# Encoder trunk on one core: moving weights of the 512-column products stored with even columns first and read as two streams

## The chip, the cores and the metric

The kernel runs on one core of a Trainium2 chip. The metric is the device time of that core in microseconds (us), from its first to its last instruction, with what little lies around them. TensorE multiplies; ScalarE (ACT in the rows), VectorE (DVE), GpSimd (POOL) and the DMA queues feed it and take its sums away.

## The reference

A trunk of two layers over 256 tokens of width 2048 with 256 memory tokens. Each layer has a token mixer with 12 heads and a cross-attention with 4 heads, one output projection, and an MLP of width 8192 with a squared ReLU. Cut to what matters here:

```python
for i in range(DEPTH):                                   # DEPTH = 2
    n = rms_norm(h, attn_norm[i])
    z = n @ a_w_in[j]     # layer 0; layer 1: n @ b_w_in[j]
    ...
    km, vm = jnp.split(m @ w_mem_kv[i], 2, axis=-1)
    ...
    h = h + jnp.concatenate([mix, cross], axis=-1) @ w_o[i]
    n = rms_norm(h, mlp_norm[i])
    h = h + jnp.square(jax.nn.relu(n @ w_up[i])) @ w_down[i]
return rms_norm(h, final_norm)
```

All of it is float32. Every dense product `n @ w` is what the change can touch; the attention itself is small beside them.

## The kernel before

Each float32 operand of a product is held as a pair, hi and lo: hi is the number rounded to float32r (a 4-byte format that TensorE multiplies in one go), lo the rest. A product is three matmuls: hi by hi, hi by lo, lo by hi. `split` (line 454; its instructions carry lines 456 and 457) makes a pair with one ACT copy and one DVE subtraction.

A matmul holds a stationary operand of 128x128 in the array and streams a moving operand through it, one column after another; each column of the moving operand gives one column of the sum in PSUM. There are two kinds of product:

- **S products** (`products`, line 350, matmul on line 362): the weights are stationary, the activations move, 256 columns (the tokens) at a time. Q and K of layer 0, the memory keys and the whole of the up projection (`up_grains`) are made so.
- **M products** (`m_products`, line 330, matmuls on lines 339, 342 and 343): 128 tokens of the activations are stationary, the weights move, 512 columns at a time. V of layer 0, the memory values, all of layer 1's input projection, the output projection and the last part of the down projection (`plain_grains`) are made so. The rest of the down projection (`down_grains`, its `run`, lines 1149, 1151 and 1152) has the same shape: it multiplies blocks by Strassen's seven products p1 to p7, with `th`/`tl` (four blocks that are sums of weights) and `bh`/`bl` (three blocks of the weights) as moving operands.

One chunk of weights is 128 partitions by 2048 columns (1 MB, `CH`), that is four blocks of 512. It is laid out on the host by `m_chunks`, `pair_chunks` and `plain_chunks`, so that a block of 512 columns lies in order in 2048 bytes of each partition. A chunk is loaded by SP's queue, split by ACT and DVE (in halves of two blocks, or four blocks `th`/`tl` and three blocks `bh`/`bl`), and read block by block by TensorE.

The constants `MOVING_AT`, `STILL_AT`, `U_AT`, `ENTRY_AT`, `LAST_AT` and so on shift single tiles by 32 to 384 bytes in the partition. The sequence of the work is set by `run_all`: a list of grains, each with a load, a preparation and a run, and with the number of grains by which load and preparation go ahead of the run. In the MLP one step is: three Strassen products with `bh`/`bl` (9 matmuls of 512 columns), an up chunk (48 matmuls of 256 columns), four Strassen products with `th`/`tl` (12 matmuls of 512). There are 58 such steps in each layer.

Two places read a moving operand that isn't one run: in layer 1's attention the keys (`Far.part`, line 132, read by lines 512 to 514) come as 8 runs of 32 columns, 512 bytes apart from start to start; and on lines 653 to 655 four runs of 64.

## Time and profile before

| | |
|---|---|
| time, median of 3 runs | 1989.95 us (1989.51 to 1990.23) |
| profiled execution, span from first to last instruction | 1988.4 us |
| TensorE busy | 1980.1 us, 100% of the span, 12838 matmuls |
| TensorE weight loads | 1799.3 us, 90% (beside the matmuls) |
| VectorE busy | 1717.0 us, 86% |
| ScalarE busy | 1339.5 us, 67% |
| GpSimd busy | 140.6 us, 7% |
| DMA engines | mean 226 GB/s |

Busy shares overlap. A matmul's record reaches from its start to the modelled end of its pipeline, so two records in a row lie over each other: the mean of 390 ns for a matmul of 512 columns isn't what it costs. What it costs is the distance from its start to the start of the next one, which the timeline view shows.

### The profile page before, as it was taken

What the parts mean: (1) busy time and instruction counts of PE and PEld (TensorE: products, weight loads), DVE (VectorE), ACT (ScalarE), POOL (GpSimd) and SP (SyncE); (2) the same over time, 40 slices, a digit from 0 to 9 for tenths busy, and PEclk for the clock granted to TensorE, in tenths of its full rate; (3) what the DMA queues carried; (4) which work ended last, traced back from release to release, by engine and by line L of the source; (5) the groups of instructions that cost most, each with busy time, mean ns of one, the idle gap of its engine ahead of it and who ended that gap; (6) DMA issues with size and microseconds to landing.
All of it is one profiled execution on the core that took longest, in us unless ns stands there. A gap on an engine that the chain in (4) does not pass through costs nothing.

```text
span 1988.4 us, 32806 instructions
## 1 busy us (share of the span) xinstructions
PE 1980.1 (100%) x12838; PEld 1799.3 (90%) x12838; DVE 1717.0 (86%) x2131; ACT 1339.5 (67%) x1892; POOL 140.6 (7%) x179
## 2 busy tenths in 40 slices
PE   9999999999999999999999999999999999999998
PEld 8999999899999999999998888889999999999997
DVE  7777777589898999999999778788998999999998
ACT  6655555477777777777766658677776777777674
POOL 0000000000000000000000001000000000000000
PEclk9999999999999999999999999999999999999999
DMA  7856655767777777777766765667777777777772
GB/s 291 320 192 207 200 192 185 270 194 241 234 234 227 230 233 238 234 227 234 216 228 204 255 226 177 207 218 250 237 223 237 226 228 236 234 238 228 225 232 111
DMA packets 117339, 448.52 MB, mean 226 GB/s; under 512 B 24640, under 2 KB 49984, under 8 KB 69824
## 3 DMA queue, kind: packets, MB, share of 16 engines
q1 hardware_dynamic: 99168, 415.12, 59.5%
q0 software_dynamic: 17728, 30.78, 9.7%
q8 instruction: 101, 1.65, 0.3%
q10 hardware_dynamic: 288, 0.52, 0.1%
q14 instruction: 54, 0.44, 0.1%
HBM read 397.78 MB, written 4.19 MB: 202 GB/s over the span
## 4 chain that ended last, share of the span: by engine, by line
PE 99%; issue 0%; DVE 0%; POOL 0%; DVEq 0%; ACT 0%; POOLq 0%; ACTq 0%
PE ps_u L362 35%; PE ps_s L362 10%; PE p L1149 9%; PE p L1152 9%; PE p L1151 9%; PE ps_m L343 8%; PE ps_m L339 8%; PE ps_m L342 8%; PE av L653 0%; PE sc_ps L513 0%; PE av L654 0%; PE sc_ps L514 0%; PE sc_ps L512 0%; PE av L655 0%; PE idle L236 0%
## 5 line engine op out<-in xcount | busy, mean ns | idle before, releaser
L362 PE MATMUL ps_u<-hT,uh 128*128 128x256 f32 x3812 | 662.9, 276 | 0.0
L362 PEld LDWEIGHTS ps_u<-hT,uh 128*128 128x128 f32 x3812 | 578.7, 188 | 5.5
L362 PE MATMUL ps_u<-hT,ul 128*128 128x256 f32 x1960 | 541.5, 276 | 0.0
L456 ACT ACTIVATE uh<-raw_U 128x1024 fp32r<-128x1024 f32 x262 | 276.8, 1058 | 208.0 <-PE ps_u L362 193.1
L362 PEld LDWEIGHTS ps_u<-hT,ul 128*128 128x128 f32 x1960 | 368.0, 188 | 0.0
L457 DVE TENSOR_TENSOR lo<-raw,hi 128x1024 fp32r<-128x1024 f32 (+1 forms) x215 | 254.3, 1189 | 92.2 <-ACT hi L456 91.1
L457 DVE TENSOR_TENSOR ul<-raw_U,uh 128x1024 fp32r<-128x1024 f32 x262 | 318.9, 1221 | 16.2 <-ACT uh L456 16.2
L457 DVE TENSOR_TENSOR tl<-t,th 128x2048 fp32r<-128x2048 f32 x116 | 265.7, 2290 | 70.4 <-ACT th L456 70.0
L456 ACT ACTIVATE hi<-raw 128x1024 fp32r<-128x1024 f32 (+1 forms) x215 | 222.0, 1038 | 143.0 <-PE ps_m L343 73.9
L456 ACT ACTIVATE th<-t 128x2048 fp32r<-128x2048 f32 x116 | 222.8, 1920 | 117.4 <-PE p L1152 112.5
L457 DVE TENSOR_TENSOR bl<-b,bh 128x1536 fp32r<-128x1536 f32 x116 | 203.3, 1753 | 0.0
L1149 PE MATMUL p<-th,a_s 128*128 128x512 f32 x464 | 181.3, 391 | 0.0
L1118 POOL DMA_DIRECT2D t<-b x116 | 100.6, 868 | 1139.4 <-ACT t L1117 1057.7
L1151 PE MATMUL p<-tl,a_s 128*128 128x512 f32 x464 | 181.0, 390 | 0.0
L1152 PE MATMUL p<-th,a_s 128*128 128x512 f32 x464 | 180.6, 389 | 0.0
L456 ACT ACTIVATE bh<-b 128x1536 fp32r<-128x1536 f32 x116 | 172.3, 1485 | 7.8
L362 PE MATMUL ps_s<-nT,hi 128*128 128x256 f32 x896 | 154.7, 277 | 0.0
L1152 PE MATMUL p<-bh,a_s 128*128 128x512 f32 x348 | 136.2, 391 | 0.0
L362 PEld LDWEIGHTS ps_s<-nT,hi 128*128 128x128 f32 x896 | 135.5, 188 | 0.1
L1149 PE MATMUL p<-bh,a_s 128*128 128x512 f32 x348 | 135.4, 389 | 0.0
L1151 PE MATMUL p<-bl,a_s 128*128 128x512 f32 x348 | 135.4, 389 | 0.0
L362 PE MATMUL ps_s<-nT,lo 128*128 128x256 f32 x448 | 124.2, 277 | 0.0
(303 smaller groups left out, 3591.0 us busy)
## 6 DMA issues: line engine op xcount, KB each, us to landing
raw_U<-in_w_up SPq DMA_DIRECT2D x128, 1024.0 KB, 5.8
b<-in_w_pair SPq DMA_DIRECT2D x116, 1024.0 KB, 5.8
raw<-in_w_o SPq DMA_DIRECT2D x32, 1024.0 KB, 5.0
t<-b POOLq DMA_DIRECT2D x116, 256.0 KB, 5.1
raw<-in_w_b SPq DMA_DIRECT2D x21, 1024.0 KB, 5.9
raw<-in_w_av SPq DMA_DIRECT2D x12, 1024.0 KB, 5.0
raw<-in_w_aq SPq DMA_DIRECT2D x12, 1024.0 KB, 4.9
raw<-in_w_ak SPq DMA_DIRECT2D x12, 1024.0 KB, 4.9
```

The costliest lines, as they stand in the source:

```text
L339: first = nc.tensor.matmul(ps, ah, hi[:, s], start=st, stop=False)
L342: nc.tensor.matmul(ps, ah, lo[:, s], start=False, stop=False)
L343: final = nc.tensor.matmul(ps, al, hi[:, s], start=False, stop=sp)
L362: ins = nc.tensor.matmul(ps, x, acts[:, k, part], start=k == n == 0, stop=k == KT - 1 and n == 2)
L456: first = nc.scalar.activation(dst_hi, src, AF.Copy)
L457: return first, nc.vector.tensor_tensor(dst_lo, src, dst_hi.bitcast(F32), op=ALU.subtract)
L1118: nc.gpsimd.dma_start(s[:, 3, :], b[:, 1, :], accum_op=ALU.add)
L1149: ins = nc.tensor.matmul(ps, a[:, 0, ai, :], hi[:, s], start=begins, stop=False)
L1151: nc.tensor.matmul(ps, a[:, 0, ai, :], lo[:, s], start=False, stop=False)
L1152: nc.tensor.matmul(ps, a[:, 1, ai, :], hi[:, s], start=False, stop=ends)
```

## The change

The three host functions that lay out moving weights store each block of 512 columns with its even columns first: place i of the block holds column 2i, place 256 + i holds column 2i + 1 (`evens_first`). The matmuls read the block by `in_turn`: place 0, place 256, place 1, place 257, and so on, so that the columns come to the array in their old order, 0, 1, 2, 3, and the sums in PSUM lie where they lay. The access pattern of the moving operand was one run of 512 elements of 4 bytes; it is now 256 times two elements, 1024 bytes apart, 4 bytes further each time. `pairs` gives PSUM's side the same shape; in the program that is built it is still one run of 512.

All 4524 matmuls of 512 columns are changed, and the 48 of 256 columns with which the last block of the kernel is made in two parts (`part`). S products, splits, loads, tile places and sizes are as before, and every engine has the same instructions in the same order with the same names.

```diff
+    def pairs(x):
+        return x.rearrange("p (i b) -> p i b", b=2)
+
+    def in_turn(x, begin=0, end=512):
+
+        return x.rearrange("p (b i) -> p i b", b=2)[:, begin // 2 : end // 2, :]
+
...
-        ps = w.ps[i if bank is None else bank][:, part[0] : part[1]]
+        ps = pairs(w.ps[i if bank is None else bank][:, part[0] : part[1]])
         for j in range(nk):
-            s = slice(j * 512 + part[0], j * 512 + part[1])
+            mh, ml = (in_turn(x[:, j * 512 : (j + 1) * 512], *part) for x in (hi, lo))
             ah, al = acts(k0 + j, i)
             st, sp = begins and j == 0, ends and j == nk - 1
-            first = nc.tensor.matmul(ps, ah, hi[:, s], start=st, stop=False)
+            first = nc.tensor.matmul(ps, ah, mh, start=st, stop=False)
             if keep_order:
                 pin(first)
-            nc.tensor.matmul(ps, ah, lo[:, s], start=False, stop=False)
-            final = nc.tensor.matmul(ps, al, hi[:, s], start=False, stop=sp)
+            nc.tensor.matmul(ps, ah, ml, start=False, stop=False)
+            final = nc.tensor.matmul(ps, al, mh, start=False, stop=sp)
...
-                ps, s = box["ps"][name], slice(bi * 512, (bi + 1) * 512)
-                ins = nc.tensor.matmul(ps, a[:, 0, ai, :], hi[:, s], start=begins, stop=False)
+                ps = pairs(box["ps"][name])
+                mh, ml = (in_turn(x[:, bi * 512 : (bi + 1) * 512]) for x in (hi, lo))
+                ins = nc.tensor.matmul(ps, a[:, 0, ai, :], mh, start=begins, stop=False)
                 pin(ins)
-                nc.tensor.matmul(ps, a[:, 0, ai, :], lo[:, s], start=False, stop=False)
-                nc.tensor.matmul(ps, a[:, 1, ai, :], hi[:, s], start=False, stop=ends)
+                nc.tensor.matmul(ps, a[:, 0, ai, :], ml, start=False, stop=False)
+                nc.tensor.matmul(ps, a[:, 1, ai, :], mh, start=False, stop=ends)
...
+def evens_first(x):
+
+
+    return x.reshape(*x.shape[:-1], 256, 2).swapaxes(-1, -2).reshape(x.shape)
...
-    return np.ascontiguousarray(x).reshape(-1, P, CH)
+    return np.ascontiguousarray(evens_first(x)).reshape(-1, P, CH)
```

The last pair of lines is from `m_chunks`; `pair_chunks` and `plain_chunks` are changed in the same way.

## Rows read from the trace of the kernel before

**Rows 1.** The page's head: span, busy times, the chain that ended last.

```profile
span 1988.4 us, 32806 instructions
PE 1980.1 (100%) x12838; PEld 1799.3 (90%) x12838; DVE 1717.0 (86%) x2131; ACT 1339.5 (67%) x1892; POOL 140.6 (7%) x179
PE 99%; issue 0%; DVE 0%; POOL 0%; DVEq 0%; ACT 0%; POOLq 0%; ACTq 0%
```

**Rows 2.** Whom TensorE waited for: line waiting, releaser, total us, times, longest.

```profile
PE idle L236 <- POOL mhalf L231: 1.0, 1, 1.0
```

**Rows 3.** Whole span, matmuls of line 1149, then of line 339 (window, its length, busy (count)).

```profile
0.00:1988.40 1988.40, 316.69 (x812) 152.58 (x812) 1.00 0.70 226
...
0.00:1988.40 1988.40, 269.53 (x712) 133.68 (x712) 1.00 0.70 226
```

**Rows 4.** Groups of TensorE, forms of line 339 with 256 columns (count, busy, mean).

```profile
L339 PE MATMUL ps_m<-uh,a_s 128*128 128x256 f32 x8 | 2.2, 280 | 0.0
L339 PE MATMUL ps_m<-h_p,a_p 128*128 128x256 f32 x8 | 2.2, 279 | 0.0
```

**Rows 5.** Timeline of TensorE, an MLP step's 21 Strassen matmuls (start us, length, line).

```profile
950.72 0.40 PE L1149 MATMUL p<-th,a_s 128*128 128x512 f32 x1
950.95 0.39 PE L1151 MATMUL p<-tl,a_s 128*128 128x512 f32 x1
951.18 0.39 PE L1152 MATMUL p<-th,a_s 128*128 128x512 f32 x1
...
955.26 0.40 PE L1152 MATMUL p<-bh,a_s 128*128 128x512 f32 x1
955.50 0.28 PE L362 MATMUL ps_u<-hT,u 128*128 128x256 f32 x1
```

**Rows 6.** Timeline of TensorE, 24 matmuls of an up chunk, first and next after.

```profile
444.17 0.39 PE L362 MATMUL ps_u<-hT,uh 128*128 128x256 f32 x2
...
446.89 0.39 PE L362 MATMUL ps_u<-hT,uh 128*128 128x256 f32 x2
```

**Rows 7.** Timeline of TensorE, layer 1: 24 matmuls with `Far` keys, moving in 8 runs.

```profile
1194.04 0.28 PE L512 MATMUL sc_ps<-kT,qT 128*128 128x256 f32 x1
...
1196.91 0.40 PE L343 MATMUL ps_m<-hi,nT 128*128 128x512 f32 x1
```

**Rows 8.** Timeline of TensorE, layer 0: 4 matmuls with memory keys in one run.

```profile
111.46 0.28 PE L514 MATMUL sc_ps<-km,qmT 128*128 128x256 f32 x1
...
111.93 0.28 PE L362 MATMUL ps_s<-nT,hi 128*128 128x256 f32 x1
```

**Rows 9.** Timeline of TensorE, start: 20 plain float32 matmuls of 128 columns.

```profile
0.98 4.63 PE L236 MATMUL idle<-ones 128*128 128x128 f32 x20 [0.98 <-POOL mhalf L231]
5.27 0.70 PE L362 MATMUL ps_s<-memT,hi 128*128 128x256 f32 x2
```

**Rows 10.** Groups of VectorE: transposes by input pattern, and splits (count, busy, mean ns).

```profile
L492 DVE STREAM_TRANSPOSE rows<-mem_col 128x256 f32<-128x256 f32 x1 | 0.4, 447 | 0.0
L565 DVE STREAM_TRANSPOSE sc_t<-sc 128x256 f32<-128x256 f32 x40 | 23.2, 618 | 0.6 <-ACT sc L526 0.6
L547 DVE STREAM_TRANSPOSE h_t<-h_t 128x512 f32<-128x512 f32 x8 | 8.2, 1103 | 0.0
L457 DVE TENSOR_TENSOR ul<-raw_U,uh 128x1024 fp32r<-128x1024 f32 x262 | 318.9, 1221 | 16.2 <-ACT uh L456 16.2
L457 DVE TENSOR_TENSOR tl<-t,th 128x2048 fp32r<-128x2048 f32 x116 | 265.7, 2290 | 70.4 <-ACT th L456 70.0
```

**Rows 11.** Stretches of the MLPs: length, busy PE, PEld, DVE, ACT, POOL, clock, DMA.

```profile
500.00:960.00 460.00, 460.00 (x3105) 422.38 (x3105) 424.24 (x436) 329.44 (x386) 40.05 (x46) 1.00 0.74 232
970.00:1030.00 60.00, 60.00 (x404) 54.98 (x403) 59.51 (x67) 42.65 (x52) 4.35 (x5) 1.00 0.73 231
1400.00:1900.00 500.00, 500.00 (x3373) 459.04 (x3373) 462.57 (x478) 358.00 (x421) 42.24 (x49) 1.00 0.74 231
1900.00:1970.00 70.00, 70.00 (x426) 62.44 (x425) 68.70 (x78) 44.48 (x57) 2.58 (x3) 1.00 0.54 182
```

**Rows 12.** Timeline of VectorE in that step: the split of `th`.

```profile
955.60 2.29 DVE L457 TENSOR_TENSOR tl<-t,th 128x2048 fp32r<-128x2048 f32 x1 [1.18 <-ACT th L456]
```

More of the change, by code (lines that the diff above doesn't have):

```diff
@@ L1588, in pair_chunks @@
     x = x.reshape(-1, 2, P, 4, 512)[:, :, :, [3, 0, 2, 1]]
-    return np.ascontiguousarray(x).reshape(-1, P, CH)
+    return np.ascontiguousarray(evens_first(x)).reshape(-1, P, CH)
 def plain_chunks(w):
@@ L1595, in plain_chunks @@
     x = [x[nb, c] for nb in REST for c in chunks_left(nb)]
-    return np.ascontiguousarray(np.stack(x)).reshape(-1, P, CH)
+    return np.ascontiguousarray(evens_first(np.stack(x))).reshape(-1, P, CH)
 def by_feature(x):
```

## The prediction

> **What bounds the kernel now.** I read the head of the page first, then the list of TensorE's waits, then the timeline. TensorE is busy in the whole span, the chain that ended last is TensorE for 99% of it [rows 1], and the only wait listed for it is 1.0 us at the start [rows 2]. So no other engine sets the time; the sum of the distances between matmul starts does. The question is then what one matmul costs, and a mean duration doesn't tell it, since records overlap. The timeline does: in one MLP step 20 matmuls of 512 columns lie between the starts 950.72 and 955.26 [rows 5], which is 4.54 / 20 = 0.2270 us for each. An up chunk's 24 matmuls of 256 columns take 446.89 - 444.17 = 2.72 us [rows 6], 113.3 ns each.
>
> The granted clock in the stretches of the MLP is 1.00, which is the 2.4 GHz level [rows 11]. One column in each cycle would be 512 / 2.4 = 213.3 ns and 256 / 2.4 = 106.7 ns. Both shapes lose the same share: 227.0 / 213.3 = 1.064 and 113.3 / 106.7 = 1.062, or one cycle for every 16 columns (17/16 = 1.0625). The loss grows with the columns, so it isn't a price of starting a matmul nor of a weight load, of which there is one for either shape. It sits in the stream of columns. The 20 plain float32 matmuls at the start go from 0.98 to 5.27 [rows 9], 214.5 ns for 128 columns, which is 512 whole cycles of 2.4 GHz and 1.2 ns: four cycles for a column, and no seventeenth (that would be 226.7). There a column of 4 bytes is wanted only every fourth cycle; here every cycle. So I take the loss for one of reading the moving operand: the reader can't quite bring 4 bytes per partition in each cycle. That is an inference from two rates, not something a row says.
>
> **What the change does, part by part.** No instruction is added, removed or moved, and no DMA: the host stores the same bytes in another order. The splits of ACT and DVE read and write the same runs. What changes is how 4572 matmuls read: 3 x 812 in the Strassen part and 3 x 712 in the other M products [rows 3], of which 3 x 16 = 48 have 256 columns [rows 4]. That leaves 4524 with 512 columns, 4524 x 0.2270 = 1027 us, 52% of the span. A nanosecond more or less on each is 4.5 us, or 0.23%.
>
> No row of the trace shows a moving operand read from two places in turn, so its price has to be bounded from both sides. The lower end is one column per cycle, 213.3 ns: the stream can't be faster than the array takes it, which excludes more than a gain of 13.7 ns. The upper end is what VectorE pays when each element lies in another place: its transposes that read elements 16 bytes apart take 1103 ns for 512 and 618 for 256, so 1.89 ns for each [rows 10], where its split takes (2290 - 1221) / 1024 = 1.04 ns for an element in a run [rows 10]. At 1.89 ns a block of 512 takes 970 ns, 743 ns more than now. In between lies TensorE's own nearest row, the one on jumps: keys in 8 runs of 32 columns, 512 bytes apart, take 2.87 / 24 = 119.6 ns [rows 7], keys in one run (111.93 - 111.46) / 4 = 117.5 ns [rows 8]. Seven jumps cost 2.1 ns at most, 0.3 ns each, less than a cycle. The reader thus follows the pattern of the instruction and not the neighbourhood in memory, and a far line costs it about what the next line costs.
>
> I take a value near the lower end. If a far line is as good as the next one, what loses the seventeenth cycle is that the next piece of a single run isn't there in time: it is wanted 16 columns after the last. With two streams in turn each piece lasts twice as long, and the piece that follows it has twice the time to come. For this the reader has to keep one piece of each stream at hand while it takes from the other. That is the weak point of the forecast; nothing above shows that it can.
>
> The sum: 4524 x (227.0 - 213.3) = 62 us at most. From it come off: (a) a fixed price of a start, now hidden in the lost cycles perhaps, 1.2 ns by the plain matmuls [rows 9], 4524 x 1.2 = 5 us. (b) VectorE as the next bound. In the steady part of the MLP it is busy 424.24 of 460 us and 462.57 of 500 [rows 11], 92%. A step of 48 x 113.3 + 21 x 227.0 = 10.2 us gets 21 x 12.5 = 0.26 us shorter, 2.6%, and VectorE's share goes to 95%: it still fits. The tightest link, `tl`, ends at 955.60 + 2.29 = 957.89 [rows 12], and its product starts 48 x 113.3 ns after 955.50 [rows 5], at 960.94: 3 us of cover, of which the change takes a tenth or so. But at the end of each layer VectorE is full: 59.51 of 60 us and 68.70 of 70 [rows 11]. There TensorE can't go faster than VectorE, so the gain of those 130 us is lost at worst, 2.6% to 5.5% of it (the higher in the part with M products alone), 4 us. ACT has more room (329 of 460). So -62 + 5 + 4 = -53 us on the profiled execution's 1988.4 us, and on the median of 1989.95, which lies 1.6 us above that span: 1937 us.
>
> For one matmul of 512 columns on an undisturbed array the Trainium skill ("TensorE: Matmul & The Clock Gate", section "Wait — 56ns, not 53.3ns?") states 215.7 ns from start to start; the trace has 227.0 here. By that page the saving would be 11.3 ns each, 51 us, and the time some 1943 us after (b), an estimate that the rest doesn't need.
>
> **The rivals.** *S, slower: each column is fetched anew.* If the reader holds one piece only, two streams in turn make it fetch at every column what it now fetches once for several. What speaks for it is VectorE's 1.89 against 1.04 ns [rows 10]: elements from another place each time cost 1.8 times as much there. Against it: VectorE never returns to a piece that it had, while here the next column but one is its neighbour; and the jumps cost TensorE nearly nothing [rows 7, 8]. The price: at double the present 227 ns (one column for two that a fetch now brings) 4524 x 227 = 1027 us more, about 3017 us; at VectorE's 1.89 ns 4524 x 743 = 3361 us more, 5350 us. It decides the sign as soon as a column costs more than 227.0 / 512 = 0.443 ns.
>
> The Trainium skill speaks for S: by "SBUF — State Buffer" (the box on cachelines in the section on the DMA port swizzle) a read that crosses to another 16-byte line than the one before pays a penalty, and full bandwidth wants two hits in a row on a line. By that rule every column here would pay. VectorE's rows agree with it for 16-byte steps; no row here shows it for TensorE.
>
> *N, nothing: the seventeenth cycle stays.* If it isn't the reader that loses it (writing sums, or a beat between two clocks), or both streams come to the end of their pieces together and each loses as before, the time is the old one, 1990 us. For it speaks that the rate is so rigid: the two shapes agree within 0.2%, wherever in the kernel. A mixed case, where one of two losses is hidden, gives half of the gain, -28 us, 1962 us; I count it with the faster ones.
>
> **How the numbers follow.** Faster, whole or half of the gain: 0.62. N: 0.18. S: 0.20. The predicted time is that of the whole gain, 1937 us. The range goes down to the whole bound with nothing given back, 1989.95 - 62 - 2 = 1926 us (2 for a start here and there that gets cheaper), and up through the half gain to N with a measurement's width, 1994 us. It leaves S out, 2 in 10. About 0.2% is what a measurement of this kernel can tell from no change, 4 us; the faster cases and N lie apart by far more than that.
>
> **What would show it.** Start to start of the Strassen matmuls: near 214 to 216 ns if right, 227 if N, 440 and more if S; the up chunk's 113.3 ns stays in every case. VectorE's share in 500 to 960 goes to about 95%, and the first real waits of TensorE appear near the ends of the layers, on splits. If the distance falls as forecast but the time doesn't, then step (b) was wrong. If the distance is right in some M products and not in others, the place of the tiles matters, which I left out.

## The result, and the profile after

The changed kernel takes 1959.1 us (median of four runs, 1956.9 to 1959.9) against 1989.8 us for the kernel before (median of four): a ratio of 0.9842, 95% interval 0.9828 to 0.9856. That is 31 us faster, in the way that was forecast, but 22 us short of the forecast 1937 us. The profiled execution is the fastest of the four; its span is 1954.8 us, 33.6 us under that of before.

The page's head, and the list of whom TensorE waited for (line waiting, releaser, total us, times, longest). These answer to [rows 1] and [rows 2]:

```profile
span 1954.8 us, 32802 instructions
PE 1935.8 (99%) x12838; PEld 1806.8 (92%) x12838; DVE 1728.7 (88%) x2131; ACT 1335.7 (68%) x1892; POOL 140.7 (7%) x179
PE 86%; DVE 6%; DMA 3%; issue 2%; ACT 2%; SPq 1%; POOL 0%; DVEq 0%; POOLq 0%; ACTq 0%
```

```profile
PE av L660 <- ACT pT_t L463: 4.3, 3, 2.4
PE ps_m L349 <- DVE lo L464: 3.6, 3, 1.9
PE av L661 <- DVE pT_t L464: 1.2, 3, 0.6
PE idle L236 <- POOL mhalf L231: 1.0, 1, 1.0
PE ps_m L349 <- DVE ul L464: 0.5, 1, 0.5
PE ps_m L349 <- DVE l_p L464: 0.5, 1, 0.5
```

The chain that ended last was TensorE for 99% [rows 1] and is now 86%, with VectorE and transfers in it. The one wait at the start [rows 2] has company: `av` (the attention's products, line 660 and 661) waits for `pT_t`, the transposed scores, and M products (line 349) wait for the low halves of weights that VectorE makes.

What one matmul costs is read from the starts. The timeline of TensorE in an MLP step, as in [rows 5] (start us, length, line, operation):

```profile
901.53 0.38 PE L1157 MATMUL p<-th,a_s 128*128 128x512 f32 x1
...
905.84 0.38 PE L1160 MATMUL p<-bh,a_s 128*128 128x512 f32 x1
906.06 0.28 PE L369 MATMUL ps_u<-hT,u 128*128 128x256 f32 x1
```

Twenty matmuls from 901.53 to 905.84 are 4.31 / 20 = 215.5 ns each, where before they were 227.0. Comparing the two traces matmul by matmul (distance to the next start, in the same order in both) gives the account of the 33.6 us:

| what | us |
|---|---|
| 4544 distances of the changed matmuls (47 of them of 256 columns) that no stall touches, mean 226.4 to 214.8 ns | -52.7 |
| distances that grew or shrank by over 40 ns, nearly all of them new waits | +15.6 |
| 7860 distances of S matmuls (256 columns), mean 113.8 to 114.2 ns | +3.3 |
| the rest | +0.2 |

(Without the 47 short ones the means are 227.5 and 215.9.) So the products gave what they should, and 16 us of it went into waits. Where these lie shows when the program is cut by the number of the matmul:

| matmuls | what | before, us | after, us |
|---|---|---|---|
| 2785 to 6500 | MLP of layer 0, steady part | 540.5 | 529.2 |
| 6500 to 7000 | its end | 75.5 | 74.1 |
| 7000 to 7250 | layer change: last down products, norm, first projections of layer 1 | 51.2 | 53.0 |
| 7250 to 8400 | layer 1: projections, attention, output projection | 236.0 | 236.0 |
| 8750 to 12250 | MLP of layer 1, steady part | 517.7 | 506.3 |
| 12250 to the end | its end | 95.5 | 92.7 |

The MLPs keep their gain to their last matmul. From 7000 to 8400 there are 1116 matmuls of 512 columns, 1116 x 11.3 = 12.6 us shorter, and the stretch became 1.7 us longer: 14.1 of the 15.6 us of waits lie there, 0.9 in layer 0 and 0.2 at the end of each MLP. The windows of the changed kernel (window, its length, busy PE, PEld, DVE, ACT, POOL with counts, clock, DMA): steady MLP, its end as in [rows 11], a piece of the layer change, and a piece around the output projection's last products:

```profile
490.00:940.00 450.00, 450.00 (x3107) 424.61 (x3107) 423.64 (x436) 329.99 (x388) 39.76 (x46) 1.00 0.76 237
940.00:1010.00 70.00, 70.00 (x481) 65.71 (x481) 68.89 (x78) 50.95 (x62) 5.62 (x7) 1.00 0.74 232
...
1035.00:1050.00 15.00, 15.00 (x71) 13.15 (x70) 15.00 (x18) 9.36 (x17) 0.00 (x0) 1.00 0.49 155
...
1285.00:1300.00 15.00, 13.07 (x61) 11.14 (x60) 14.45 (x17) 12.00 (x21) 0.73 (x1) 1.00 0.60 151
```

VectorE is at 94% in the steady MLP, as forecast. At the MLP's end it is at 68.89 of 70 us and TensorE still has no gap: it works ahead there. In the layer change it is full, and around 1285 TensorE has lost 1.93 us of 15. The longest wait for a low half shows why. First VectorE, then TensorE, in the timeline:

```profile
1287.92 5.87 DVE L554 STREAM_TRANSPOSE h_t<-h_t 128x512 f32<-128x512 f32 x4
1293.71 2.53 DVE L554 STREAM_TRANSPOSE h_s<-h_s 128x512 f32<-128x512 f32 x2
1296.17 2.31 DVE L464 TENSOR_TENSOR lo<-raw,hi 128x1024 fp32r<-128x1024 f32 x2
```

```profile
1294.88 0.59 PE L346 MATMUL ps_m<-hi,cat 128*128 128x512 f32 x2
1297.41 0.48 PE L349 MATMUL ps_m<-lo,cat 128*128 128x512 f32 x1 [1.93 <-DVE lo L464]
```

The subtraction that TensorE needs stands behind six transposes on VectorE, 1296.17 - 1287.92 = 8.2 us of them. In the kernel before the same six took 1313.41 - 1307.44 = 6.0 us:

```profile
1307.44 4.12 DVE L547 STREAM_TRANSPOSE h_t<-h_t 128x512 f32<-128x512 f32 x4
1311.43 2.12 DVE L547 STREAM_TRANSPOSE h_s<-h_s 128x512 f32<-128x512 f32 x2
1313.41 2.37 DVE L457 TENSOR_TENSOR lo<-raw,hi 128x1024 fp32r<-128x1024 f32 x2
```

The difference of 2.3 us is more than the wait of 1.93 us. It isn't peculiar to this place: VectorE's transposes, which the change doesn't touch, are longer in the changed kernel, 85.3 us in all where they took 67.7. Two groups of them over the whole span, which took 1103 and 618 ns before [rows 10]:

```profile
L554 DVE STREAM_TRANSPOSE h_t<-h_t 128x512 f32<-128x512 f32 x8 | 11.7, 1527 | 0.0
L572 DVE STREAM_TRANSPOSE sc_t<-sc 128x256 f32<-128x256 f32 x40 | 29.0, 763 | 0.6 <-ACT sc L533 0.6
```

Taken one by one, the 21 of `sc_t` that ran while TensorE read in turn took 789 to 874 ns, and the 11 that ran beside other matmuls 593 to 644; in the kernel before all 40 took 585 to 641. VectorE's subtractions of 128x1024 took 1215 and 1216 ns in the two cases. So the new way of reading makes another engine's instructions longer, the transposes, which read elements 16 bytes apart. From matmul 7000 to 8400 there are 52 of them, 55.4 us in place of 41.7: 13.7 us more on VectorE, where TensorE's new waits are 14.1 us. (VectorE's busy time there, in which transposes in a row overlap a little, grew by 10.7 us.)

### The profile page after: what moved, and what is told of

The parts are those of the page before. It is cut to its first block, busy times and chain, and to the rows that moved or that the text cites. A ratio compares the mean times of both kernels' runs of the same rounds, so it can differ in the third digit from the quotient of the medians.

```text
span 1954.8 us, 32802 instructions
## 1 busy us (share of the span) xinstructions
PE 1935.8 (99%) x12838; PEld 1806.8 (92%) x12838; DVE 1728.7 (88%) x2131; ACT 1335.7 (68%) x1892; POOL 140.7 (7%) x179
## 4 chain that ended last, share of the span: by engine, by line
PE 86%; DVE 6%; DMA 3%; issue 2%; ACT 2%; SPq 1%; POOL 0%; DVEq 0%; POOLq 0%; ACTq 0%
PE ps_u L369 36%; PE ps_s L369 10%; PE p L1159 9%; PE p L1157 9%; PE p L1160 9%; PE ps_m L350 4%; PE ps_m L349 4%; PE ps_m L346 4%; DVE lo L464 1%; DMA pT_t<-sc_t 1%; SPq L577 1%; DVE sc_t L572 1%; ACT hi L463 1%; SPq L557 1%; DMA raw_U<-in_w_up 0%
## 5 line engine op out<-in xcount | busy, mean ns | idle before, releaser
L464 DVE TENSOR_TENSOR ul<-raw_U,uh 128x1024 fp32r<-128x1024 f32 x262 | 318.8, 1220 | 13.7 <-ACT uh L463 9.0
L464 DVE TENSOR_TENSOR tl<-t,th 128x2048 fp32r<-128x2048 f32 x116 | 265.6, 2290 | 51.2 <-ACT th L463 50.6
L1160 PE MATMUL p<-th,a_s 128*128 128x512 f32 x464 | 175.9, 379 | 0.0
L1159 PE MATMUL p<-tl,a_s 128*128 128x512 f32 x464 | 175.7, 379 | 0.0
L1157 PE MATMUL p<-th,a_s 128*128 128x512 f32 x464 | 175.7, 379 | 0.0
L1160 PE MATMUL p<-bh,a_s 128*128 128x512 f32 x348 | 131.9, 379 | 0.0
L1157 PE MATMUL p<-bh,a_s 128*128 128x512 f32 x348 | 131.9, 379 | 0.0
```

Of the source, the lines that this page charges most:

```text
L464: return first, nc.vector.tensor_tensor(dst_lo, src, dst_hi.bitcast(F32), op=ALU.subtract)
L1157: ins = nc.tensor.matmul(ps, a[:, 0, ai, :], mh, start=begins, stop=False)
L1159: nc.tensor.matmul(ps, a[:, 0, ai, :], ml, start=False, stop=False)
L1160: nc.tensor.matmul(ps, a[:, 1, ai, :], mh, start=False, stop=ends)
```

## The experiments

### What a pattern costs TensorE

The first kernel measures the disputed price by itself: one stationary tile, one operand in SBUF, and 24 matmuls in a row for each way of reading it. Its patterns, in elements of 4 bytes as [step, count], the innermost last:

```diff
+    ("one", [[1, 512]]),
+    ("turnKB", [[1, 256], [256, 2]]),
...
+    ("turnOneLine", [[1, 256], [8, 2]]),
+    ("turnKBandLine", [[1, 256], [264, 2]]),
...
+    ("twice", [[1, 256], [0, 2]]),
+    ("everySecond", [[2, 512]]),
+    ("everyFourth", [[4, 512]]),
...
+    ("fourStreams", [[1, 128], [128, 4]]),
+    ("eightStreams", [[1, 64], [64, 8]]),
...
+        for n in range(N):          # 24
+            pin(nc.tensor.matmul(o, w, m, start=n == 0, stop=n == N - 1))
...
```

> A kernel that holds none of the reference's computation: it loads a tile, rounds it to float32r, and runs 24 matmuls for each of 24 read patterns of the moving operand, from the same place of the same tile, and writes sums that mean nothing. Read: start to start of one matmul by pattern. Theory A (the reader brings a piece of a run at a time, is late for the next piece by one cycle in 16 columns, and two streams give each piece twice the time): one run 227 ns; two streams in turn at any distance that puts them into different pieces 215 to 216; two streams 32 bytes apart, in the same piece for much of the time, nearer to 227; sixteen columns from each in turn (a whole piece at a time) 227 again; every second element of one run, which uses up pieces twice as fast, above 227, some 240; every element twice, half the bytes, 216. Rival B (the form of the pattern, a short inner count, is what helps, not the two places): every pattern with an inner count of 2, also two elements or sixteen from each in turn and the ones 32 bytes apart, 216; every second element, one long count, 227. Rival C (banks: the two places must or must not fall together): the distances of 32, 64, 128, 256 bytes and of 1 KB plus these differ among themselves by 5 ns or more, and 1024 is one of the good ones.

The timeline of TensorE, one row for the 24 matmuls of a pattern; what one costs is the distance from the row's start to the next row's start, over 24 (the next start of a row whose successor is left out stands in the text):

```profile
21.41 5.60 PE L69 MATMUL one<-mov,w 128*128 128x512 f32 x24
26.85 5.34 PE L69 MATMUL turnKB<-mov,w 128*128 128x512 f32 x24
32.03 5.34 PE L69 MATMUL turnHalfKB<-mov,w 128*128 128x512 f32 x24
...
52.75 5.34 PE L69 MATMUL turnOneLine<-mov,w 128*128 128x512 f32 x24
57.93 5.34 PE L69 MATMUL turnKBandLine<-mov,w 128*128 128x512 f32 x24
...
78.65 5.34 PE L69 MATMUL twice<-mov,w 128*128 128x512 f32 x24
83.83 11.04 PE L69 MATMUL everySecond<-mov,w 128*128 128x512 f32 x24
94.69 11.25 PE L69 MATMUL everyFourth<-mov,w 128*128 128x512 f32 x24
105.76 10.53 PE L69 MATMUL everyEighth<-mov,w 128*128 128x512 f32 x24
116.11 6.98 PE L69 MATMUL fourStreams<-mov,w 128*128 128x512 f32 x24
122.92 11.88 PE L69 MATMUL eightStreams<-mov,w 128*128 128x512 f32 x24
```

One run costs (26.85 - 21.41) / 24 = 226.7 ns, two streams in turn (32.03 - 26.85) / 24 = 215.8 ns. That is the change's whole effect on a matmul, on an array with nothing else to do, so the price is TensorE's own. All ten distances between the two streams, from 32 bytes to 2 KB and with or without a line more, give the same 215.8; so does reading each element twice. Every second element costs 452.5 ns and every fourth 461. Four streams in turn cost 283.8, eight (next start 134.63) 487.9. Two, four, eight and sixteen elements from each of two streams in turn cost 328, 250, 243 and 240. None of the three theories holds as it was put: A had streams 32 bytes apart nearer to 227, every second element at some 240 and sixteen at a time at 227; B had every pattern of two in turn at 216 and every second element at 227; C wanted the distances to differ.

So how far apart the streams lie plays no part, and what counts isn't the number of streams either. Seen as two half-streams, the even columns and the odd columns of the matmul, the prices fall in order: in one plain run each half-stream steps by 8 bytes; in two streams in turn, and in `twice`, by 4; in `everySecond` by 16. A second kernel tested this on patterns where the two readings part, and moved the stationary tile in its partition by 32 bytes at a time:

```diff
...
+PATTERNS += [("turnEverySecond", [[2, 256], [512, 2]], 0), ("turnEveryFourth", [[4, 256], [1024, 2]], 0),
+             ("everyThird", [[3, 512]], 0)]
+for n, a in enumerate("ABCDEFGH"):
+    PATTERNS += [("halfOne" + a, [[1, 256]], 8 * n), ("halfTurn" + a, [[1, 128], [128, 2]], 8 * n)]
...
```

> Again none of the reference's computation, 24 matmuls for each pattern. Two questions. First, what in two streams in turn is it that reads faster? Theory P (the reader brings two neighbouring elements, 8 bytes, at a time; in turn it keeps both pairs, so that each is used in full): two streams that each go in steps of two or four elements use half of every pair and take twice the time, 430 to 460 ns; two streams at distances of 1, 2, 3 or 257 elements take 216, if pairs need not begin at even places, and 227 or more at the odd ones if they must. Rival (any two-stream pattern is read in a mode of its own, one element from each in every cycle): steps of two and four within the streams also 216. Second, what does the place of the stationary operand against the moving one do? 256 columns of one run took 119 ns in the first study and 113.3 in the kernel: by the places in steps of 32 bytes one run should give 113 at some and 119 at others; two streams in turn 111.7 at all of them if the loss and this sensitivity are one and the same thing, and differ among places by 3 to 6 ns if they are two.

The same view of this kernel (the row ahead of `turnEverySecond` ends at its start):

```profile
51.59 5.63 PE L52 MATMUL turnEverySecond<-mov,w 128*128 128x512 f32 x24
57.06 11.04 PE L52 MATMUL turnEveryFourth<-mov,w 128*128 128x512 f32 x24
67.91 10.98 PE L52 MATMUL everyThird<-mov,w 128*128 128x512 f32 x24
78.71 3.06 PE L52 MATMUL halfOneA<-mov,w 128*128 128x256 f32 x24
81.61 2.84 PE L52 MATMUL halfTurnA<-mov,w 128*128 128x256 f32 x24
```

Two streams in turn that each step by 8 bytes cost (57.06 - 51.59) / 24 = 227.9 ns, as one plain run does; stepping by 16 bytes they cost 452, as `everySecond` does; every third element costs 450. Theory P wanted 430 to 460 for both steps and its rival 216, so neither holds as it was put. Two streams 4, 8 or 12 bytes apart, or 1 KB and 4 bytes, cost 215.8 to 216.4. The step of each half-stream gives the price wherever it is one step throughout: 4 bytes 215.8, 8 bytes 227, 16 bytes and more 430 to 461. The rule is not complete: in `fourStreams`, and where two or more elements are taken from each stream in turn, each half-stream jumps between two places, and the step alone doesn't give the 240 to 328 ns that this costs.

The place of the stationary tile matters for one run only. With 256 columns one run cost 120.8, 118.3, 114.6, 118.7, 119.2, 120, 117.9 and 117 ns at the eight places, two streams 111.3 to 111.7 at all of them. With 512 columns, at four of the places, one run cost 228 to 233 and two streams 215.8. (One run at the same place came out at 226.7 and at 228.0 in this kernel, so a difference of 1 or 2 ns says little.) How a plain run's reads fall out against the reads of weights thus seems to be part of its price, which reading in turn takes away; how they meet no run shows.

The Trainium skill's box on cachelines ("SBUF — State Buffer", section on the DMA port swizzle), which stood behind rival S, says that a line has 16 bytes and wants two hits in a row. Counted over all columns, as the prediction did, it is wrong here: two streams in turn change the line at each column and are the fastest. Counted in each half-stream, the three levels are four hits on a line, two and one, and the great step does lie between two and one, as that rule has it; that 4 hits are better than 2 (215.8 against 227) goes beyond it.

### Each part of the change alone

Only the Strassen products read in turn, then only the other M products. The first leaves `m_products`, `m_chunks` and `plain_chunks` as before, the second the `run` of `down_grains` and `pair_chunks`:

```diff
-        ps = pairs(w.ps[i if bank is None else bank][:, part[0] : part[1]])
+        ps = w.ps[i if bank is None else bank][:, part[0] : part[1]]
...
-            first = nc.tensor.matmul(ps, ah, mh, start=st, stop=False)
+            first = nc.tensor.matmul(ps, ah, hi[:, s], start=st, stop=False)
```

```diff
-                ps = pairs(box["ps"][name])
+                ps, s = box["ps"][name], slice(bi * 512, (bi + 1) * 512)
...
-                ins = nc.tensor.matmul(ps, a[:, 0, ai, :], mh, start=begins, stop=False)
+                ins = nc.tensor.matmul(ps, a[:, 0, ai, :], hi[:, s], start=begins, stop=False)
```

> The change in the Strassen part alone (2436 of the 4524 matmuls); all other M products as before. Theory A with the loss in the layer change and in layer 1's projections and attention: the Strassen steps had cover, so the whole gain stays, 2436 x 11.3 ns = 27.5 us, 1962 us. Rival (the fed engines, VectorE above all, limit the MLP once TensorE is faster there): a third of that or more is given back, 1971 us and up.

> The change in lines 339 to 343 alone (2088 matmuls of 512 columns); the Strassen part as before. Theory A with the loss in layer 1: 2088 x 11.3 ns = 23.6 us at the matmuls, some 16 us given back as new waits at the same places as with the whole change, so 1982 us. Rival (the loss comes from the whole kernel running ahead of its loads, and is smaller where half of it runs as before): 1966 to 1972 us.

Strassen alone: 1964.0 us, ratio 0.9871 (0.9856 to 0.9886), -25.7 us; its trace has 28.7 us of shorter distances and only 0.4 us of waits beyond the one at the start. M products alone: 1984.0 us, ratio 0.9969 (0.9959 to 0.9979), -6 us, of 24.0 us by which its matmuls are shorter. The two sum to the change. So the gain of the MLP's Strassen products is kept, and three quarters of the gain of the M products is given back; 2112 of the 4544 distances are theirs.

VectorE's transposes go with the M products. The group of `h_t` with Strassen alone, where they are as short as in the kernel before, then with the M products alone, where they are as long as with the whole change:

```profile
L554 DVE STREAM_TRANSPOSE h_t<-h_t 128x512 f32<-128x512 f32 x8 | 8.2, 1091 | 0.0
```

```profile
L554 DVE STREAM_TRANSPOSE h_t<-h_t 128x512 f32<-128x512 f32 x8 | 11.7, 1522 | 0.0
```

The second run also shows what one of these waits can bring with it. Timeline of TensorE, and the window right behind the wait (columns as above, the clock third from the end):

```profile
1240.48 0.38 PE L350 MATMUL ps_m<-hi,cat 128*128 128x512 f32 x1
1243.39 0.38 PE L660 MATMUL av<-pT_t,vb 128*128 128x256 f32 x1 [2.52 <-ACT pT_t L463]
...
1243.95 0.63 PE L349 MATMUL ps_m<-lo,cat 128*128 128x512 f32 x1
...
1246.93 0.46 PE L350 MATMUL ps_m<-hi,cat 128*128 128x512 f32 x1
```

```profile
1243.00:1248.00 5.00, 4.61 (x14) 3.79 (x15) 4.42 (x8) 3.84 (x9) 0.00 (x0) 0.66 0.81 274
```

After a gap of 2.9 us between starts seven matmuls lie 0.427 us apart, 512 columns at the 1.2 GHz level, with a granted clock of 0.66 over the window: 7 x 0.21 = 1.5 us more for one wait. (This trace is that of the longest of the nine runs; a second such stretch stands at 1312 to 1316, with a clock of 0.58.) In the profiled run of the changed kernel the gap at the same place is 2.8 us, from 1227.45 to 1230.25, and the clock stayed at 1.00; so this price is paid in some executions and not in others. It may be part of the 2 to 3 us by which the other three runs of the changed kernel, of which no trace is kept, are longer than the profiled one.

### What gives the gain back

The waits on `av` lie behind a chain: scores are transposed by VectorE (`turned`), four transfers that SyncE issues carry `sc_t` to `pT_t`, ScalarE and VectorE split it. Two rearrangements were tried first: layer 1's four transfers issued by GpSimd instead of SyncE, and the attention's last step one grain later.

```diff
-            nc.sync.dma_start(raw[:, a].rearrange("p k c -> p (k c)"),
+            (nc.gpsimd if box["layer"] else nc.sync).dma_start(raw[:, a].rearrange("p k c -> p (k c)"),
```

```diff
-                       for j, kv in enumerate(kvs)], (3, 6, 8)[blk], 2, (0, 2, 5, 9 if blk == 1 else 6))
+                       for j, kv in enumerate(kvs)], (3, 6, 8)[blk], 2, (0, 2, 5, 10 if blk == 1 else 7))
```

> The changed kernel, with layer 1's four DMAs that turn each softmax block issued on GpSimd's queue instead of SP's. Theory Q (TensorE waits for these blocks since their issues stand behind weight loads in SP's queue, which wait for a buffer): the waits of lines 660 and 661 in layer 1, some 9 us, shrink by more than half, 1952 to 1954 us. Rival R (the chain was laid out in grains, and a grain of M products is now 5% shorter than the chain needs; the queue is not late): no change, 1957 to 1960 us, or longer if GpSimd's issues take longer than the 0.6 us of SP's.

> The changed kernel, with the last step of layer 1's attention (the products with V) one grain later in the order, 7 for 6 and 10 for 9. By R this gives the chain 2.6 us more before TensorE asks for it: the 9 us of waits there go to 1 or 2, less what a longer hold of the buffers costs, 1951 to 1954 us. By Q, or if the blocks are late for another reason that moves along, as VectorE being full, 1957 us and more.

The first gave 1956.2 us (1955.1 to 1957.3), 2.9 us less than the changed kernel and between the two forecasts; the waits of `av` (5.5 us in the changed kernel's list above, where the two expectations speak of 9) fell to 4.6 us, one of 3.7 us among them. The second gave 1962.9 us (1961.5 to 1963.7), worse by 3.8: the wait of `av` fell, and the output projection behind it waited longer (37.1 us in place of 31.7 between matmuls 8250 and 8400). Shifting the chain's work only moves the wait, so something that all of these stages share had to be behind it.

The next two kernels take work from VectorE and nothing else. The low half of a 128x1024 block of weights is filled by a plain copy in place of the subtraction; first in layer 1's projections and output projection only, then in the whole kernel:

```diff
-        return first, nc.vector.tensor_tensor(dst_lo, src, dst_hi.bitcast(F32), op=ALU.subtract)
+        return first, nc.vector.tensor_copy(dst_lo, src) if light else nc.vector.tensor_tensor(dst_lo, src, dst_hi.bitcast(F32), op=ALU.subtract)
```

with `light` on line 278 for layer 1, and in the second kernel for every source of 128x1024.

> The changed kernel, but in layer 1's projections and output projection VectorE fills the low half of each 128x1024 block of weights by a plain copy instead of the difference (1.18 to 1.23 us each in the changed kernel); this leaves the low parts' values wrong and the amount of work of all other engines as it was. The program's planner moves some instructions against each other for it. Between matmuls 7250 and 8400 the changed kernel lost 2.4 us in waits for the low half (2.1 of them at one place, behind six transposes on VectorE) and about 6.3 us in waits of the attention's products (av) for ScalarE's pT_t, which itself waits for the transfer pT_t<-sc_t. Theory V (VectorE is late in these stages and everything that passes through it, the transposes in front of the transfers too, is late with it): the waits for the low half fall under 0.5 us, those of av under 2 us, and the kernel takes 1947 to 1951 us. Rival D (the way sc_t, transfer, ScalarE, av is too long by itself for the shorter products ahead of it): the waits for the low half fall, those of av stay at 5 to 7 us, 1954 to 1958 us. The layer change (7000 to 7250) is the part that is left as it was: 53.0 us under both.

> As the run with the light copy in layer 1 (1950.9 us), but every 128x1024 block of weights in the whole kernel, the layer change and the MLPs included, gets its low half by VectorE's plain copy (0.68 us in place of 1.2); the low parts' values are wrong again, all other work stays. The 512-column products are 52.7 us shorter in the changed kernel's trace, 16 us of it went into waits, 3 into longer S products. Theory V (VectorE's backlog is behind nearly all of the waits, those of the layer change too): the layer change (matmuls 7000 to 7250) falls from 53.0 to 49 to 50 us and the kernel takes 1944 to 1948 us. Rival D (the waits of the layer change come from the round of sums, norm, transposes and transfers, which a lighter split does not shorten): the layer change stays at 52 to 53 us, and the kernel at 1949 to 1952 us.

The copy takes 684 ns, the subtraction 1216 (groups of VectorE between 1070 and 1280, first of the changed kernel, then of the first light one):

```profile
L464 DVE TENSOR_TENSOR lo<-raw,hi 128x1024 fp32r<-128x1024 f32 x68 | 81.8, 1216 | 12.0 <-ACT hi L463 11.8
```

```profile
L464 DVE CAST lo<-raw 128x1024 fp32r<-128x1024 f32 x69 | 46.8, 684 | 14.9 <-PE ps_m L349 12.6 <-DMA raw<-in_w_b 2.0
```

Light in layer 1: 1950.9 us (1950.0 to 1951.8). Matmuls 7250 to 8400 take 229.4 us instead of 236.0, the waits of `av` fall from 5.5 to 1.4 us, and the layer change, which was left as it was, stays at 53.0 with its 1.6 us of waits for low halves. Light everywhere: 1945.7 us (1945.1 to 1946.3); the layer change falls to 49.1 us, and the two steady MLP parts stay at 529.2 and 506.3 us to the tenth. The list of TensorE's waits of the first, then of the second:

```profile
PE ps_m L349 <- DVE lo L464: 1.6, 2, 1.1
PE av L660 <- ACT pT_t L463: 1.1, 2, 0.7
```

```profile
PE av L660 <- ACT pT_t L463: 1.1, 2, 0.8
...
PE sc_ps L519 <- ACT sc L527: 0.7, 1, 0.7
```

No wait for a low half is left in the second, and the waits of `av` for `pT_t` on ScalarE were mostly VectorE's too, since the transposes ahead of the transfers stand in its queue. Together the lighter copies bring back 11.5 us by the spans of the profiled runs (13.4 by the medians), where the changed kernel had lost 15.6 in waits. (The planner that orders the program moved some instructions of layer 1 for them, so single waits can't be set against each other there; the sums can.) That TensorE waits because VectorE is late is thereby shown by taking work from VectorE; the MLPs, which didn't move, show that it isn't the bound where it is merely busy. Why it is late the two kernels don't show: the transposes of `h_t` stay long in them (1527 and 1546 ns), and no run has all products read in turn and the transposes short. So how much of the loss comes from the longer transposes, and how much from TensorE asking sooner, stays open.

### The same reading for the 256-column products

If one run of 256 columns costs 113 to 114 ns in the kernel and two streams 111.3 to 111.7, the S products should gain too. Their moving activations were read in turn; the sums then lie with even tokens first, and their first reader takes every second element of PSUM:

```diff
+    def by_two(x):
+        return x.rearrange("p (b i) -> p i b", b=2)
+    def ordered(ps):
+        return ps.rearrange("p (i b) -> p b i", b=2)
...
-                ins = nc.tensor.matmul(ps, x, acts[:, k, part], start=k == n == 0,
+                ins = nc.tensor.matmul(pairs(ps), x, by_two(acts[:, k, part]), start=k == n == 0,
...
-        nc.scalar.activation(two, ps, AF.Relu)
+        nc.scalar.activation(c[:, 2 * e : 2 * e + 2, :], ordered(ps), AF.Relu)
```

> The changed kernel, and the 7920 matmuls of 256 columns of the S products read their moving activations as two streams in turn as well: token i and token 128 + i; the sums come out with these two side by side, and the first reader of each sum takes them apart (every second element of PSUM: lines 507 and 1073 of the changed kernel). From the first study, 256 columns in turn take 111.7 ns for 113.3 to 114.4 now: 2.0 ns x 7920 = 16 us less at the matmuls. Theory A: most of it stays in the MLP and in layer 0, 1943 to 1948 us. Rival (reading every second element of PSUM makes ACT and VectorE slower, or VectorE has no room left at 94%): 1953 us and up.

1939.6 us (1938.9 to 1940.1), ratio 0.9749 (0.9735 to 0.9764), 19.5 us under the changed kernel and better than expected. The S matmuls' mean distance is 111.8 ns, from 114.2; the steady MLPs go to 523.4 and 500.8 us; the distances that grew come to 17.5 us, from 15.6. The transposes of 128x128 in layer 0, now beside products read in turn too, take 455 ns in the mean, from 406. This version beats both kernels.

With GpSimd issuing layer 1's four transfers as well, as above:

> The version that reads the 256-column products in turn too (1939.6 us) with layer 1's four transfers pT_t<-sc_t issued by GpSimd in place of SyncE, which by itself gave 2.9 us. If the two are independent: 1936.5 to 1938 us. If the shorter S products have moved the waits to places where the issue order of SyncE plays no part: 1939 to 1941 us.

1939.0 us (1938.3 to 1939.6), the same within the measurement: the 2.9 us didn't add up. A wait of `av` of 3.7 us stays in it, the same one that stood in the run with the transfers alone.

Last, the remedy that the light copies suggest, for real: on top of the version of 1939.6 us GpSimd makes the low half of every second block in layer 1.

```diff
-                box["weights"] = split(*tiles[hf], src)
+                box["weights"] = split(*tiles[hf], src, by=nc.gpsimd if box["layer"] and hf else nc.vector)
```

> The version that reads the 256-column products in turn too (1939.6 us), with the low half of every second 128x1024 block of layer 1's projections and output projection, 35 blocks, formed by GpSimd in place of VectorE, where it was 1.2 us a block; no row yet shows what GpSimd takes for it. The run with the light copy took 37 us from VectorE there and gave 8 us. Theory V (VectorE's backlog is what gives the gain back in these stages): if GpSimd takes up to some 3 us a block, 1932 to 1936 us, with the waits for VectorE and for pT_t in layer 1's attention mostly gone. Rival P (the blocks stay long on GpSimd, TensorE waits for them, and the 8 factors of the heads stand behind them in GpSimd's queue): 1940 to 1960 us, with TensorE's waits named after the low half on GpSimd.

1953.3 us (1949.9 to 1954.9), 13.7 us worse. The groups that tell why: GpSimd's subtractions and a two-operand group of VectorE in this kernel, then the same VectorE group in the version without it:

```profile
L470 POOL TENSOR_TENSOR lo<-raw,hi 128x1024 fp32r<-128x1024 f32 x36 | 92.2, 2561 | 106.8 <-ACT hi L469 87.9 <-issue 15.0 <-DMA pT_t<-sc_t 3.9
...
L470 DVE TENSOR_TENSOR pT_t<-pT_t 128x512 fp32r<-128x512 f32 x16 | 18.5, 1159 | 4.9 <-ACT pT_t L469 4.8
```

```profile
L470 DVE TENSOR_TENSOR pT_t<-pT_t 128x512 fp32r<-128x512 f32 x16 | 11.1, 691 | 7.1 <-ACT pT_t L469 7.1
```

GpSimd takes 2.56 us for a block, inside what theory V allowed, yet VectorE's own work got longer: the split of `pT_t` 1159 ns in place of 691, and the rotation of the heads (`b_o`, two operands) 1853 in place of 686. These are means: four of the 16 splits took 2.3 to 2.8 us and the other twelve 0.65 to 0.69. VectorE's reductions and transposes, with one operand, didn't get longer (671 ns for `nm`, 675 in the changed kernel). Of TensorE's waits in this run rival P's own, for a low half on GpSimd, is 2.7 us; those for VectorE's low halves are 5.2 us, for `b_o` 3.0 us and for `qT` on ScalarE 3.6 us. So rival P was right in the time, and half right in the reason: the two engines also stand in each other's way. That agrees with the Trainium skill ("SBUF — State Buffer", section "SBUF: two separate sides"), by which VectorE's second operand and GpSimd share a port that one of them holds for a whole instruction.

## Why the prediction was right in kind and short in size

**What bounds the kernel** was right: a matmul's distance is the price, and the change shortened it on nearly every one of the 512-column products [rows 5].

**The price of reading in turn** was right within 1.3 ns: 214.5 ns taken (213.3 and 1.2 for the start), 215.8 measured alone and 215.5 in the MLP. The trace has 52.7 us for the forecast's 62 - 5 = 57. The 215.7 ns of the Trainium skill that stood beside it ("TensorE: Matmul & The Clock Gate", section "Wait — 56ns, not 53.3ns?"), an estimate of 51 us, was nearer still: the changed kernel's trace agrees with it, the kernel before with its 227.0 didn't.

**The reason for it** held in its first half only. The lost cycle is one of reading the moving operand, as inferred from the two rates; the patterns show it with nothing else running. The picture of a piece that "lasts twice as long" with two streams didn't hold as it was put: an element read twice from one stream, and streams 32 bytes apart, are as fast, and stepping by 8 bytes in two streams is as slow as one run. What decides, in the patterns of one step, is the step of the even and of the odd columns, each by itself. "Follows the pattern of the instruction and not the neighbourhood in memory", drawn from [rows 7, 8], was wrong: those rows show that 8 jumps cost little, not that a step at each column would; with every second element the price doubles.

**Rival S** had the right price for the wrong pattern. Doubling, 227 to 452 ns, is there, when each half-stream steps by 16 bytes. Two streams in turn are the opposite case.

**Rival N** didn't come about: both reasons given for it, sums or clocks, fall with 215.8 ns on the same sums at the same clock. The rate that it called "so rigid" isn't: by the place of the stationary tile one run of 256 columns costs 114.6 to 120.8 ns.

**Step (b) is the term that was mis-sized**, and misplaced. It took VectorE as the next bound, which is right, and 4 us for it, at the ends of the MLPs (its own 2.6% to 5.5% of 130 us are 3 to 7 us). Measured: 0.2 us of waits at each of the two ends, and 14.1 us in the layer change and in layer 1's projections, attention and output projection. Three readings led there. A full VectorE was taken for a bound: at the MLP's end it is full at 68.89 of 70 us because it works ahead, and TensorE loses nothing. The stretches between the MLPs weren't looked at, since TensorE had no wait there before. This window of the kernel before, in its layer change, would have told:

```profile
1057.00:1073.00 16.00, 16.00 (x72) 13.24 (x72) 16.00 (x21) 11.61 (x23) 0.00 (x0) 1.00 0.64 195
```

VectorE was busy for all 16 us there, and TensorE without a gap only because its operands had been made ahead. And VectorE's work was taken as given, since its instructions stay the same. They do, but the transposes among them, which [rows 10] has as a price for comparison, became longer by 13.7 us in these stretches through the change itself; in the layer change (matmuls 7000 to 7250) by 3.9 us, where TensorE's waits are 3.7 us. A TensorE that runs 5% faster through 1116 products also uses up such a lead sooner; the runs don't separate the two. With VectorE's work cut the stretch from 7000 to 8400 goes from 289.0 us (53.0 + 236.0) to 279.0 us, the sum of the parts of the run that was light everywhere, against 287.2 before.

**A term that was missing**: "the up chunk's 113.3 ns stays in every case". The S matmuls, not touched, became longer by 0.4 ns in the mean, 3.3 us. That one run of 256 columns depends on places is shown by the second pattern kernel; why it is a little more so in the changed kernel isn't settled.

The terms then add up: 1989.95 - 52.7 + 15.6 + 3.3 + 0.2 = 1956.4 us by the traces, the time of the profiled run (1956.9); the other runs are 2 to 3 us longer, at a mean clock of 0.997 to 0.998. The measured time lies well inside the stated range, but that range reached from the whole gain to none; the forecast itself was 22 us off.

## What to carry to other kernels

Price an operand's access pattern by measuring it alone, 24 matmuls in a row for each pattern: float32r read as two streams in turn cost 215.8 ns for 512 columns where one run cost 226.7, and every second element 452. When a bound engine gets faster, look for the next bound in the stretches where another engine is already full and the first is only covered by a lead, not where the shares are merely high; and test it by making that engine's work lighter before building a remedy. Set the durations of the other engines' instructions against those before, also of the ones that the change leaves alone: here the transposes became up to 1.5 times as long and nothing in the diff says so. Moving elementwise work from VectorE to GpSimd was no remedy here, where VectorE's instructions beside it have two operands in SBUF.

## What the runs showed of the hardware

- TensorE reads the even and the odd columns of a float32r operand like two streams, as far as the patterns with one step go: 215.8, 227 and 430 to 461 ns for 512 columns as each steps by 4, 8, or 16 and more bytes; the distance between them, from 4 bytes to 2 KB, costs 0.6 ns at most.
- VectorE's transposes, which read 16 bytes apart, get longer while TensorE reads in turn: 128x256 from 621 to 837 ns in the mean, 128x512 from 1.1 to 1.5 us. VectorE's subtractions beside the same matmuls don't.
- One run's price depends on where the stationary tile lies, in steps of 32 bytes: 114.6 to 120.8 ns for 256 columns. In turn it is 111.3 to 111.7 everywhere.
- Four streams in turn cost 284 ns, eight 488: more streams are not better.
- The same gap of 2.8 to 2.9 us between two matmuls left the granted clock at 1.00 in one run and was followed by seven matmuls at the 1.2 GHz level in another.
- With 36 subtractions on GpSimd, two groups of VectorE's two-operand instructions became 1.7 and 2.7 times as long in the mean (691 to 1159 ns, 686 to 1853 ns): four of 16 and four of six took 2.3 to 2.8 us, the others what they took before.
